# One sequence for neighbourhood and latent attention heads on TensorE, and a token-wise norm for the latent key

## The chip, the cores and the metric

The kernel runs on one core of a Trainium2 chip. The metric is device time in microseconds (us) of one execution; lower is better. The time before is the median of three runs. A profile is one more execution with the hardware profiler on; times in it are counted from the start of its span. Engines are named as in the profile: PE (TensorE matmul), PEld (its weight loads), DVE (VectorE), ACT (ScalarE), POOL (GpSimd), SP (SyncE, which here only issues DMAs).

## The reference, cut to what matters

One encoder layer over 512 tokens with 1024 features. The part that the change touches is the attention: a neighbourhood attention with 8 heads and a latent attention with 8 heads, both fed from one layer-normed input `h`.

```
z = h @ W_in          # columns: NA q | NA k | NA v | c_q (384) | c_kv (256) | k_rope (32)
a_na  = neighbourhood_attention(q_na, k_na, v_na, rpb)        # 8 heads of 64, window 8 x 16, plus bias
q     = rms_norm(c_q, q_norm_g) @ w_uq                        # 8 heads of 64 + 32 (the 32 rotated)
kv    = rms_norm(c_kv, kv_norm_g) @ w_ukv                     # 8 heads of 64 (key) + 64 (value)
a_mla = softmax(concat(q_nope, rope(q_rope)) . concat(k_nope, rope(k_r)) * 96**-0.5) @ v
h     = LN1(alpha * h + concat(a_na, a_mla) @ W_o)
# rms_norm(x, g) = x * rsqrt(mean(x^2) + eps) * g, over the features of a token
```

After it come an expert layer (PEER), a gate and a second LayerNorm, which the change leaves alone.

## The kernel before, in words

Activations lie transposed, features on the 128 partitions and the 512 tokens along the free axis. Every float32 operand of a large product is kept as a high and a low part, and `mm3` (L90 to L92) issues three matmuls for one product. `split` (L75, L76; with a scale L78, L79) makes the two parts: a cast on ScalarE, then a subtraction on VectorE. `stream` loads a weight block through SP's DMA queue into one of three `raw` buffers and splits it into one of two `whi`/`wlo` buffers.

The attention stage's pieces:

- `latent_k(0)`, `latent_k(1)`: the latent key's two halves of 128 features, their squares added up. `rope_key`: the rotated 32-feature key, 24 matmuls and three VectorE operations. `latent_k_norm`: a product with a matrix of ones sums the squares over the partitions and gives every partition the same 512 sums (L298); then VectorE refines the inverse root over 128 x 512 (L300 to L305, four steps of `rsqrt_refine`, L96 to L99), multiplies both halves with it and splits them into `ckh`, `ckl`.
- `na_proj(m)`, m = 0 to 3: queries and keys of a pair of neighbourhood heads, 16 steps of three matmuls. `latent_q(i)`, i = 0 to 2: 8 steps each, with squares added into `sq_q`. `latent_q_scale`: the sums of `sq_q` by token (L330) and their inverse roots `rq`, `nrq`. `latent_values`: 8 steps; it also puts the rotated key into place with DMAs on POOL's queue and clears rows with POOL's memsets.
- `mla_proj(m)`, m = 0 to 3: queries and keys of a pair of latent heads, 5 steps, and before an even m `rope_q`, 6 steps, whose result goes into place by DMAs on POOL's queue.

`run_heads` writes TensorE's order out by hand. It goes over 32 units (pair m, block of 128 queries b, head hh) as a pipeline: in iteration i it issues the scores of unit i + 2, then some steps of the `feeds` (the generators above), then the transposition of unit i's probabilities (L191), and after every second unit the product with the values. The number of feed steps per iteration is the rate: 2.5 (`FEED_NA`) for the neighbourhood heads, 1.2 (`FEED_LAT`) for the latent ones. A feed has a due pair: what is due is driven to its end right before that pair's first scores. A generator's last operations, such as the splits, are issued only when the next step is asked for.

There are two calls of `run_heads`, one for the neighbourhood heads and one for the latent heads; both stand in regions in which TensorE's order is kept as written. `mla_proj(0)` stands between them, outside. The other engines' orders are chosen by the scheduler.

Memory that matters here: PSUM banks come from pools, two banks named `pj` (all projections), two `mm` (scores), two `tr`, two `hp` (head products, and every third latent score). A new tile waits until the bank's last reader is done. `p_exp` and `p_t` have four buffers each in SBUF. The pool `p1` holds the neighbourhood stage's values, bias tiles and projections; after it is closed, `w2h`/`w2l` (half of `W_o`) and the rotated queries `qrh`/`qrl` take its room.

Of the kernel before, what the change touches and what calls it, by code (L numbers as in the profile page):

```python
# [51 lines left out]
def tile_encoder_layer(ctx: ExitStack, tc: tile.TileContext, A: dict, out: bass.AP):  # L52
# [140 lines left out]
        nc.scalar.copy(pT[:, :nk], ps[:, :nk])  # L193
        return pT

    def run_heads(scores, product, feeds, rate, nk):

        ids = [(m, b, hh) for m in range(4) for b in range(4) for hh in range(2)]  # L200
        probs, pts = {}, {}
        fed = 0.0

        def step():
            while feeds:
                if next(feeds[0][1], feeds) is not feeds:
                    return True
                feeds.pop(0)
            return False

        for i in range(-2, len(ids) + 1):
            if i + 2 < len(ids):
                u = ids[i + 2]
                while feeds and feeds[0][0] <= u[0] and step():
                    pass
                probs[u] = scores(*u)
            fed += rate
            while fed >= 1:
                step()
                fed -= 1  # L220
            if 0 <= i < len(ids):
                pts[ids[i]] = transposed(probs.pop(ids[i]), nk)
            if i >= 2 and i % 2 == 0:
                m, b, _ = ids[i - 1]
                product(m, b, [pts.pop((m, b, hh)) for hh in range(2)])
        while step():
            pass

# [64 lines left out]
            nc.vector.tensor_tensor(sq, sq, lat[-1][1], op=OP.add)  # L293
        lat.append((cg, sq))

    def latent_k_norm(lat):
        ss = ps_tile("pj")
        nc.tensor.matmul(ss, ones, lat[-1][1], start=True, stop=True)  # L298
# [4 lines left out]
        nc.vector.reciprocal(sd, sd)  # L303
# [21 lines left out]

    def latent_q_scale():

        ss = ps_tile("pj")
        for c in range(4):
            nc.tensor.matmul(ss[:, c:c + 1], sq_q[:, c * 128:(c + 1) * 128], ones[:, 0:1], start=True, stop=True)  # L330
        yield
        ve = small.tile([128, 4], F32, name="q_ve")
        nc.vector.tensor_scalar(ve, ss[:, 0:4], 1.0 / 384, EPS, op0=OP.mult, op1=OP.add)
        sd = small.tile([128, 4], F32, name="q_sd")
        nc.scalar.sqrt(sd, ve)
        nc.vector.reciprocal(sd, sd)
        rsqrt_refine(rq, sd, ve, ve)
        nc.vector.tensor_scalar(nrq, rq, -(QD ** -0.5), None, op0=OP.mult)
        nc.vector.tensor_scalar(rq, rq, QD ** -0.5, None, op0=OP.mult)

    def rope_key():
        w = stream(A["w_kr"].rearrange("(k p) n -> p k n", p=128), [8, 64])
# [87 lines left out]
                yield  # L430
            nc.scalar.copy(v_mla[:, c, :], ps)

    feeds = []
    for m in range(1, 4):
        feeds += [(m, na_proj(m)), (4, latent_q(m - 1))]
    feeds += [(4, latent_q_scale()), (4, latent_values())]
    with tc.manual_schedule(engines={nc.tensor.engine}):
        lat_k = []
        for part in (latent_k(0, lat_k), latent_k(1, lat_k), na_proj(0), rope_key()):
            for _ in part:  # L440
# [7 lines left out]
    ow = p3.enter_context(tc.tile_pool(name="ow", bufs=1))  # L448
    w2h = ow.tile([128, 8, 512], F32R, name="w2h")
    w2l = ow.tile([128, 8, 512], F32R, name="w2l")  # L450
    p2 = ExitStack()
    lw = p2.enter_context(tc.tile_pool(name="lw", bufs=1))

    qrh = [lw.tile([128, T], F32R, name=f"qrh{r}") for r in range(2)]
    qrl = [lw.tile([128, T], F32R, name=f"qrl{r}") for r in range(2)]

    def q_proj(ps, w, off):
        for k in range(3):
# [4 lines left out]
    def rope_q(r):  # L463
        w = stream(A["w_qr"][:, r * 256:(r + 1) * 256].rearrange("(k p) n -> p k n", p=128), [3, 256])
        px, py = ps_tile("pj"), ps_tile("pj")
        yield from q_proj(px, w, 0)
        yield from q_proj(py, w, 128)
        t1 = lw.tile([128, T], F32, name="qr_t1")
        t2 = lw.tile([128, T], F32, name="qr_t2")
        nc.vector.tensor_tensor(t1, px, cosT, op=OP.mult)  # L470
        nc.vector.tensor_tensor(t2, py, sinT, op=OP.mult)
        nc.vector.tensor_tensor(t1, t1, t2, op=OP.add)
        split(qrh[r], qrl[r], t1)

    def mla_proj(m):
        if m % 2 == 0:
            yield from rope_q(m // 2)
        b = m % 2
        w = stream(A["w_qn"][:, m * 128:(m + 1) * 128].rearrange("(k p) n -> p k n", p=128), [3, 128])
        psq = ps_tile("pj")  # L480
        yield from q_proj(psq, w, 0)
        w = stream(A["w_uk"][:, m * 128:(m + 1) * 128].rearrange("(k p) n -> p k n", p=128), [2, 128])
        psk = ps_tile("pj")
        for k in range(2):
            mm3(psk, (w[0][:, k], w[1][:, k]), (ckh[:, k, :], ckl[:, k, :]), k == 0, k == 1)
            yield
        for par in range(2):
# [9 lines left out]
    n_sc = 0  # L497
# [30 lines left out]
    def load_w2():  # L528
        for kk in range(4):
            raw = wst.tile([128, 2, 512], F32, name="raw", bufs=3)  # L530
            nc.sync.dma_start(raw, A["w_o"][kk * 256:(kk + 1) * 256, 512:1024].rearrange("(k p) n -> p k n", p=128))
            split(w2h[:, 2 * kk:2 * kk + 2], w2l[:, 2 * kk:2 * kk + 2], raw)
        yield

    for _ in mla_proj(0):
        pass
    with tc.manual_schedule(engines={nc.tensor.engine}):
        run_heads(mla_scores, mla_product, [(m, mla_proj(m)) for m in range(1, 4)] + [(4, load_w2())], FEED_LAT, 512)
    p2.close()


    lnp = p3.enter_context(tc.tile_pool(name="lnp", bufs=1))
    lg = row_bcast(lnp, A["ln1_g"], "lg")
# [491 lines left out]
```

## Time and profile before

| | |
|---|---|
| median of 3 runs | 1671.72 us (1669.95 to 1673.59) |
| the profiled execution's own time | 1672.38 us |
| its span, first to last instruction | 1670.6 us |
| mean granted TensorE clock | 0.990 |
| PE, DVE, ACT, POOL busy | 96%, 79%, 44%, 23% |
| first neighbourhood scores, first latent scores | at 73.93 us, at 194.45 us |

A row of the timeline has start, duration, engine, line, operation, what is written from what, shapes, count, and in brackets the engine's idle time before it with what ended it. A row of the waits has who waited, for whom, and total, count and longest in us. Matmul rows show 0.39 us for a 512-column matmul, but they overlap: the next starts 0.23 us later at full clock. The granted clock is given as a share of full speed. Idle time of an engine costs only where TensorE, which is busy nearly all the time, has to wait for it.

### The profile page before, as it was taken

How to read it: one execution, taken by the hardware profiler on the slowest of the kernel's cores; microseconds unless marked ns; L12 is line 12 of the kernel's file. 1: busy time of each engine (PE TensorE's matmuls, PEld its weight loads, DVE VectorE, ACT ScalarE, POOL GpSimd, SP SyncE). 2: the span in 40 equal slices, each digit the busy share in tenths (PEclk: the TensorE clock that was granted, in tenths of full speed). 3: DMA queues.
4: the chain of work that ended last, by engine and by line, in shares of the span. 5: the costliest groups of instructions: out<-in, count | busy, mean ns of one | idle time of the engine just before them, and what ended most of it. 6: DMA issues, size and time to landing. Idle time of an engine off the chain costs nothing.

```text
span 1670.6 us, 24127 instructions
## 1 busy us (share of the span) xinstructions
PE 1611.0 (96%) x8539; PEld 1423.1 (85%) x8539; DVE 1324.9 (79%) x2869; ACT 730.7 (44%) x1233; POOL 383.4 (23%) x335
## 2 busy tenths in 40 slices
PE   6998899999999999999999999999999999999997
PEld 4777777788778999998999999999999999988886
DVE  7466685689999999967878787887878878867776
ACT  3355675433257486753333333333333333333343
POOL 1013100000000000014434343443444434432200
PEclk9999999999999999999999999999999999999999
DMA  7232141233236554479989999899898998977773
GB/s 223 59 107 77 50 143 38 92 90 88 101 124 214 192 192 176 166 267 340 342 319 325 306 333 342 287 340 319 296 334 306 329 337 306 322 251 255 261 240 116
DMA packets 180888, 376.05 MB, mean 225 GB/s; under 512 B 13216, under 2 KB 99616, under 8 KB 177696
## 3 DMA queue, kind: packets, MB, share of 16 engines
q1 hardware_dynamic: 141216, 234.52, 41.5%
q0 software_dynamic: 39552, 140.00, 24.1%
q8 instruction: 67, 1.10, 0.3%
q14 instruction: 53, 0.43, 0.1%
HBM read 339.61 MB, written 32.51 MB: 223 GB/s over the span
## 4 chain that ended last, share of the span: by engine, by line
PE 82%; DVE 12%; ACT 2%; issue 2%; DMA 1%; SPq 0%; POOL 0%; ACTq 0%; DVEq 0%
PE acc L90 10%; PE acc L92 10%; PE acc L91 10%; PE hp L92 10%; PE hp L90 9%; PE hp L91 9%; PE tr L779 3%; PE mm L90 3%; PE mm L92 3%; PE mm L91 3%; PE pj L91 3%; PE pj L90 3%; PE pj L92 3%; DVE oh_j L774 2%; DVE wlo L76 2%
## 5 line engine op out<-in xcount | busy, mean ns | idle before, releaser
L92 PE MATMUL hp<-hTh,wlo 128*128 128x384 f32 x1024 | 349.3, 341 | 5.1 <-DVE wlo L76 5.1
L90 PE MATMUL hp<-hTh,whi 128*128 128x384 f32 x1024 | 349.2, 341 | 2.3 <-ACT ge L609 2.3
L91 PE MATMUL hp<-hTl,whi 128*128 128x384 f32 x1024 | 348.4, 340 | 0.0
L849 POOL DMA_INDIRECT gat<-in_u_rows_dram,i_sel x128 | 170.6, 1333 | 630.8 <-issue 425.3
L92 PE MATMUL acc<-v_hi,a_lo 128*128 128x512 f32 x756 | 294.5, 390 | 0.0
L90 PE MATMUL acc<-v_hi,a_hi 128*128 128x512 f32 x756 | 294.3, 389 | 0.0
L91 PE MATMUL acc<-v_lo,a_hi 128*128 128x512 f32 x756 | 294.2, 389 | 0.0
L75 ACT CAST whi<-raw 128x1024 fp32r<-128x1024 f32 (+3 forms) x181 | 184.4, 1019 | 234.5 <-PE hp L91 121.0
L76 DVE TENSOR_TENSOR wlo<-raw,whi 128x1024 fp32r<-128x1024 f32 (+3 forms) x181 | 213.1, 1180 | 63.0 <-ACT whi L75 62.5
L75 ACT CAST v_hi<-v_raw 128x1024 fp32r<-128x1024 f32 x126 | 132.4, 1051 | 272.2 <-issue 229.6
L860 POOL DMA_INDIRECT gat<-in_v_rows_dram,i_sel x128 | 174.7, 1365 | 267.4 <-DVE base L862 241.2
L76 DVE TENSOR_TENSOR v_lo<-v_raw,v_hi 128x1024 fp32r<-128x1024 f32 x126 | 154.2, 1224 | 83.5 <-ACT v_hi L75 83.4
L92 PEld LDWEIGHTS hp<-hTh,wlo 128*128 128x128 f32 x1024 | 193.3, 189 | 7.7 <-DVE wlo L76 7.7
L90 PEld LDWEIGHTS hp<-hTh,whi 128*128 128x128 f32 x1024 | 193.3, 189 | 6.0 <-ACT ge L609 2.6
L91 PEld LDWEIGHTS hp<-hTl,whi 128*128 128x128 f32 x1024 | 193.2, 189 | 3.4
L862 DVE SCALAR_TENSOR_TENSOR base<-gat,hdot,base 128x1024 f32<-128x1024 f32 x128 | 164.0, 1282 | 10.7 <-DMA gat<-in_v_rows_dram,i_sel 8.4
L92 PEld LDWEIGHTS acc<-v_hi,a_lo 128*128 128x128 f32 x756 | 142.1, 188 | 30.4 <-DVE a_lo L76 1.3
L851 DVE SCALAR_TENSOR_TENSOR scr<-gat,h 128x1024 f32<-128x1024 f32 x128 | 156.4, 1222 | 12.9 <-DMA gat<-in_u_rows_dram,i_sel 10.6
L91 PEld LDWEIGHTS acc<-v_lo,a_hi 128*128 128x128 f32 x756 | 142.1, 188 | 26.3
L90 PEld LDWEIGHTS acc<-v_hi,a_hi 128*128 128x128 f32 x756 | 141.5, 187 | 26.5 <-ACT a_hi L75 0.7
L75 ACT CAST a_hi<-ge 128x384 fp32r<-128x384 f32 x112 | 57.5, 513 | 211.0 <-DVE ge L918 211.0
L76 DVE TENSOR_TENSOR a_lo<-ge,a_hi 128x384 fp32r<-128x384 f32 x112 | 62.6, 559 | 71.2 <-ACT a_hi L75 71.2
(325 smaller groups left out, 2466.9 us busy)
## 6 DMA issues: line engine op xcount, KB each, us to landing
raw<-in_uT_dram SPq DMA_DIRECT2D x128, 512.0 KB, 6.4
v_raw<-in_v_rows_dram SPq DMA_DIRECT2D x128, 512.0 KB, 6.7
g_dram<-g_st SPq DMA_DIRECT2D x24, 1024.0 KB, 4.5
gt<-g_dram SPq DMA_DIRECT2D x16, 1536.0 KB, 15.1
raw<-in_w_in_dram SPq DMA_DIRECT2D x17, 512.0 KB, 4.0
raw<-in_w_q_dram SPq DMA_DIRECT2D x16, 512.0 KB, 4.1
na_b<-in_na_bias_dram POOLq DMA_DIRECT2D x32, 128.0 KB, 2.3
raw<-in_w_o_dram SPq DMA_DIRECT2D x8, 512.0 KB, 4.8
```

The source lines that it names most:

```text
L75: nc.scalar.copy(hi, src)
L76: nc.vector.tensor_tensor(lo, src, r32(hi), op=OP.subtract)
L90: nc.tensor.matmul(ps, a[0], b[0], start=start, stop=False)
L91: nc.tensor.matmul(ps, a[0], b[1], start=False, stop=False)
L92: nc.tensor.matmul(ps, a[1], b[0], start=False, stop=stop)
L774: nc.vector.tensor_scalar(oj[:, i], iota, eT[:, 1, t0 + i:t0 + i + 1], eT[:, 2, t0 + i:t0 + i + 1], op0=OP.is_equal, op1=OP.mult)
L779: nc.tensor.matmul(ps[:, i * 128:(i + 1) * 128], oj[:, 4 * r + i, :], oi[:, 4 * r + i, :], start=True, stop=True)
L849: nc.gpsimd.indirect_dma_start(out=u[:], out_offset=None, in_=u_rows, in_offset=bass.IndirectOffsetOnAxis(ap=i_sel[:, c, k:k + 1], axis=0))
L851: nc.vector.scalar_tensor_tensor(scr, u, 1.0, h[c], op0=OP.mult, op1=OP.mult, accum_out=hdot[:, c, k:k + 1])
L860: nc.gpsimd.indirect_dma_start(out=u[:], out_offset=None, in_=v_rows, in_offset=bass.IndirectOffsetOnAxis(ap=i_sel[:, c, k:k + 1], axis=0))
L862: nc.vector.scalar_tensor_tensor(base[c], u, hdot[:, c, k:k + 1], base[c], op0=OP.mult, op1=OP.add)
```

## The change

- The two calls of `run_heads` become one over 64 units, first the neighbourhood kind, then the latent kind. The rates become 2.75 and 1.0. `mla_proj(0)` is now a feed like the others, due before the first latent scores. At iteration 32 `p1` is closed and `w2h`, `w2l` are allocated.
- `latent_k_norm` sums the squares by token (`token_sums`, four products with one column), refines the inverse root on a 128 x 4 tile (`rms_refined`, now shared with the query's norm), writes it onto the diagonals of four 128 x 128 blocks, and a product with ones (L325) spreads it over the partitions; the two halves are multiplied with it straight from PSUM. It is cut in two: its first part stands before `rope_key`, its second behind it.
- `latent_values` stands before `latent_q_scale`, no longer after it.
- The rotated queries live in `aTh`/`aTl` (blocks 6 and 7) until the heads' results overwrite them; `rope_q`'s first product goes to a `p_exp` buffer and its second is multiplied in its PSUM bank. The first three latent scores take `mm` banks.

The core of the diff:

```diff
-FEED_NA = 2.5
-FEED_LAT = 1.2
+FEED_NA = 2.75
+FEED_LAT = 1.0
...
-    def run_heads(scores, product, feeds, rate, nk):
-        ids = [(m, b, hh) for m in range(4) for b in range(4) for hh in range(2)]
+    def run_heads(kinds, feeds, at_unit):
+        ids = [(kd, m, b, hh) for kd in range(len(kinds)) for m in range(4) for b in range(4) for hh in range(2)]
...
-                while feeds and feeds[0][0] <= u[0] and step():
+                while feeds and feeds[0][0] <= 4 * u[0] + u[1] and step():
                     pass
-                probs[u] = scores(*u)
-            fed += rate
+                probs[u] = kinds[u[0]][0](*u[1:])
+            fed += kinds[ids[max(0, min(i, len(ids) - 1))][0]][3]
...
+            if i in at_unit:
+                at_unit[i]()
...
-    def latent_k_norm(lat):
-        ss = ps_tile("pj")
-        nc.tensor.matmul(ss, ones, lat[-1][1], start=True, stop=True)
-        ve = aw.tile([128, T], F32, name="p_t", bufs=4)
-        nc.vector.tensor_scalar(ve, ss, 1.0 / 256, EPS, op0=OP.mult, op1=OP.add)
-        sd = aw.tile([128, T], F32, name="p_t", bufs=4)
+    def rms_refined(ss, width):
+        ve = small.tile([128, 4], F32, name="rms_ve")
+        nc.vector.tensor_scalar(ve, ss[:, 0:4], 1.0 / width, EPS, op0=OP.mult, op1=OP.add)
+        sd = small.tile([128, 4], F32, name="rms_sd")
         nc.scalar.sqrt(sd, ve)
         nc.vector.reciprocal(sd, sd)
-        rsqrt_refine(sd, sd, ve, ve)
+        y = small.tile([128, 4], F32, name="rms_y")
+        rsqrt_refine(y, sd, ve, ve)
+        return y
+
+    def token_sums(sq):
+        ss = ps_tile("pj")
+        for c in range(4):
+            nc.tensor.matmul(ss[:, c:c + 1], sq[:, c * 128:(c + 1) * 128], ones[:, 0:1], start=True, stop=True)
+        return ss
+
+    def latent_k_norm(lat):
+        y = rms_refined(token_sums(lat[-1][1]), 256)
+        dg = aw.tile([128, T], F32, name="p_t", bufs=4)
+        for c in range(4):
+            nc.vector.tensor_scalar(dg[:, c * 128:(c + 1) * 128], ident, y[:, c:c + 1], None, op0=OP.mult)
+        yield
+        bc = ps_tile("pj")
+        nc.tensor.matmul(bc, ones, dg, start=True, stop=True)
         for i, (cg, _) in enumerate(lat):
-            nc.vector.tensor_tensor(cg, cg, sd, op=OP.mult)
+            nc.vector.tensor_tensor(cg, cg, bc, op=OP.mult)
             split(ckh[:, i, :], ckl[:, i, :], cg)
+        yield
...
+    qrh, qrl = [aTh[:, 6 + r] for r in range(2)], [aTl[:, 6 + r] for r in range(2)]
...
-        t1 = lw.tile([128, T], F32, name="qr_t1")
-        t2 = lw.tile([128, T], F32, name="qr_t2")
+        t1 = aw.tile([128, T], F32, name="p_exp", bufs=4)
         nc.vector.tensor_tensor(t1, px, cosT, op=OP.mult)
-        nc.vector.tensor_tensor(t2, py, sinT, op=OP.mult)
-        nc.vector.tensor_tensor(t1, t1, t2, op=OP.add)
+        nc.vector.tensor_tensor(py, py, sinT, op=OP.mult)
+        nc.vector.tensor_tensor(t1, t1, py, op=OP.add)
...
-        ps = psH.tile([128, 512], F32, name="hp") if n_sc % 3 == 2 else ps_tile("mm")
+        ps = psH.tile([128, 512], F32, name="hp") if n_sc % 3 == 2 and n_sc > 2 else ps_tile("mm")
...
-    feeds += [(4, latent_q_scale()), (4, latent_values())]
...
-        for part in (latent_k(0, lat_k), latent_k(1, lat_k), na_proj(0), rope_key()):
-        latent_k_norm(lat_k)
-        run_heads(na_scores, na_product, feeds, FEED_NA, NA_KEYS)
-    p1.close()
...
-    for _ in mla_proj(0):
-        pass
-        run_heads(mla_scores, mla_product, [(m, mla_proj(m)) for m in range(1, 4)] + [(4, load_w2())], FEED_LAT, 512)
+    feeds += [(4, latent_values()), (4, latent_q_scale())]
+    feeds += [(4 + m, mla_proj(m)) for m in range(4)] + [(8, load_w2())]
...
+        for part in (latent_k(0, lat_k), latent_k(1, lat_k), na_proj(0)):
+            for _ in part:
+                pass
+        norm = latent_k_norm(lat_k)
+        next(norm)
+        for _ in rope_key():
+            pass
+        next(norm)
+        run_heads([(na_scores, na_product, NA_KEYS, FEED_NA), (mla_scores, mla_product, 512, FEED_LAT)], feeds,
+                  {32: na_done})
```

More of the change, by code (lines that the diff above doesn't have):

```diff
@@ L326, in latent_q_scale @@
     def latent_q_scale():
-        ss = ps_tile("pj")
-        for c in range(4):
-            nc.tensor.matmul(ss[:, c:c + 1], sq_q[:, c * 128:(c + 1) * 128], ones[:, 0:1], start=True, stop=True)
+        ss = token_sums(sq_q)
         yield
[L332 to L339, printed above, removed]
+        y = rms_refined(ss, 384)
+        nc.vector.tensor_scalar(nrq, y, -(QD ** -0.5), None, op0=OP.mult)
+        nc.vector.tensor_scalar(rq, y, QD ** -0.5, None, op0=OP.mult)
     def rope_key():
@@ L431, in latent_values @@
             nc.scalar.copy(v_mla[:, c, :], ps)
-    feeds = []
-    for m in range(1, 4):
-        feeds += [(m, na_proj(m)), (4, latent_q(m - 1))]
-    feeds += [(4, latent_q_scale()), (4, latent_values())]
-    with tc.manual_schedule(engines={nc.tensor.engine}):
-        lat_k = []
-        for part in (latent_k(0, lat_k), latent_k(1, lat_k), na_proj(0), rope_key()):
-            for _ in part:
-                pass
-        latent_k_norm(lat_k)
-        run_heads(na_scores, na_product, feeds, FEED_NA, NA_KEYS)
-    p1.close()
-    p3 = ExitStack()
[L448 to L455, printed above, removed]
+    qrh, qrl = [aTh[:, 6 + r] for r in range(2)], [aTl[:, 6 + r] for r in range(2)]
+    p3 = ExitStack()
+    late_tiles = {}
     def q_proj(ps, w, off):
@@ L486, in mla_proj @@
             yield
+        assert m < 2 or n_sc >= 8 * (m - 1), "the tiles still hold an earlier pair"
         for par in range(2):
@@ L495, in mla_proj @@
                 split(st[par, b][0][rows], st[par, b][1][rows], ps[rows])
-    n_sc = 0
     def mla_scores(m, c, par):
@@ L531, in load_w2, with na_done @@
             nc.sync.dma_start(raw, A["w_o"][kk * 256:(kk + 1) * 256, 512:1024].rearrange("(k p) n -> p k n", p=128))
[L532 removed]
+            split(late_tiles["w2h"][:, 2 * kk:2 * kk + 2], late_tiles["w2l"][:, 2 * kk:2 * kk + 2], raw)
         yield
[L535 to L539 removed]
+    def na_done():
+        p1.close()
+        ow = p3.enter_context(tc.tile_pool(name="ow", bufs=1))
+        for n in ("w2h", "w2l"):
+            late_tiles[n] = ow.tile([128, 8, 512], F32R, name=n)
+    feeds = []
+    for m in range(1, 4):
+        feeds += [(m, na_proj(m)), (4, latent_q(m - 1))]
+    feeds += [(4, latent_values()), (4, latent_q_scale())]
+    feeds += [(4 + m, mla_proj(m)) for m in range(4)] + [(8, load_w2())]
+    with tc.manual_schedule(engines={nc.tensor.engine}):
+        lat_k = []
+        for part in (latent_k(0, lat_k), latent_k(1, lat_k), na_proj(0)):
[8 more added lines that the diff above has]
+                  {32: na_done})
+    w2h, w2l = late_tiles["w2h"], late_tiles["w2l"]
     lnp = p3.enter_context(tc.tile_pool(name="lnp", bufs=1))
```

7 lines of the change are left out of this document (4 added, 3 removed).

## The prediction

> **What bounds the kernel now.** I read the page's engine shares and chain first, then busy time by stretches over the attention stage (cut where TensorE's behaviour changes), then TensorE's waits there, then the timeline around each long wait.
>
> ```profile
> PE 1611.0 (96%) x8539; PEld 1423.1 (85%) x8539; DVE 1324.9 (79%) x2869; ACT 730.7 (44%) x1233; POOL 383.4 (23%) x335
> PE 82%; DVE 12%; ACT 2%; issue 2%; DMA 1%; SPq 0%; POOL 0%; ACTq 0%; DVEq 0%
> ...
> 67.80:92.40 24.60, 18.84 (x77) 13.55 (x75) 19.06 (x39) 10.99 (x20) 2.15 (x4) 0.86 0.24 64
> 92.40:125.30 32.90, 32.90 (x198) 28.27 (x196) 20.50 (x70) 18.03 (x48) 6.45 (x12) 1.00 0.38 110
> 125.30:162.70 37.40, 34.14 (x193) 28.20 (x191) 22.49 (x65) 17.66 (x43) 10.12 (x20) 1.00 0.26 79
> 162.70:174.40 11.70, 6.25 (x30) 5.36 (x29) 7.32 (x20) 5.91 (x12) 4.18 (x9) 0.71 0.25 63
> 174.40:193.10 18.70, 18.70 (x109) 15.65 (x107) 9.38 (x29) 11.50 (x28) 0.51 (x2) 1.00 0.08 21
> 193.10:240.00 46.90, 42.81 (x286) 33.03 (x286) 40.91 (x95) 35.60 (x73) 7.30 (x15) 1.00 0.37 100
> ```
>
> The columns of the stretches are length, then busy time (and count) of PE, PEld, DVE, ACT, POOL, then the granted clock, DMA share and GB/s. TensorE is the bound: 96% busy, 82% of the chain. The change touches only 68 to 240 us. TensorE idles there in four of six stretches, and in two of them the clock falls below 1.00. What follows is bound by TensorE too, so I count what is won here one for one. TensorE's waits from 60 to 240 us, total, times, longest:
>
> ```profile
> PE pj L330 <- DVE sq_q L321: 5.5, 1, 5.5
> PE tr L191 <- DVE p_exp L186: 5.4, 1, 5.4
> PE mm L91 <- DVE na_kl L76: 1.8, 2, 1.1
> PE pj L90 <- DVE hTl L76: 1.8, 2, 1.4
> PE mm L90 <- ACT na_kh L75: 1.4, 2, 0.7
> PE mm L90 <- ACT hTh L75: 1.3, 1, 1.3
> PE tr L191 <- DVE rs L185: 0.6, 1, 0.6
> PE pj L90 <- DVE p_exp L348: 0.3, 1, 0.3
> PE mm L92 <- DMA hTl<-qrl: 0.3, 1, 0.3
> ```
>
> Together 18.4 us. The two long ones leave a half clock behind them; here are those stretches, and a feeding step (three matmuls) slow and fast:
>
> ```profile
> 86.00:92.00 6.00, 5.58 (x17) 4.60 (x18) 4.84 (x14) 3.16 (x7) 0.54 (x1) 0.50 0.34 97
> 170.00:175.00 5.00, 5.00 (x20) 4.31 (x21) 1.48 (x9) 1.54 (x4) 0.00 (x0) 0.56 0.01 3
> 88.83 0.63 PE L90 MATMUL pj<-hTh,whi 128*128 128x512 f32 x1
> 90.11 0.63 PE L90 MATMUL pj<-hTh,whi 128*128 128x512 f32 x1
> 96.05 0.40 PE L90 MATMUL pj<-hTh,whi 128*128 128x512 f32 x1
> 96.75 0.39 PE L90 MATMUL pj<-hTh,whi 128*128 128x512 f32 x1
> ```
>
> A step takes 1.28 us after the wait and 0.70 us normally. The half clock costs 5.58 x 0.50 = 2.8 us and 5.00 x 0.44 = 2.2 us. All that can be won is 18.4 + 5.0 = 23.4 us, less what the new order costs in waits of its own.
>
> **Part 1: the norm and the first transpose.** The first transposition waits 5.4 us because VectorE is busy with the latent key's norm over 512 columns:
>
> ```profile
> 67.89 0.40 PE L90 MATMUL pj<-hTh,whi 128*64 128x512 f32 x1
> 73.47 1.02 PE L298 MATMUL pj<-p_exp,ones 128*128 128x512 f32 x2
> 86.42 0.69 PE L191 MATMUL tr<-ident,p_exp 128*128 128x128 f32 x2 [5.41 <-DVE p_exp L186]
> 169.73 1.87 PE L330 MATMUL pj<-ones,sq_q 128*128 128x1 f32 x8 [5.45 <-DVE sq_q L321]
> 68.98 1.22 DVE L76 TENSOR_TENSOR wlo<-raw,whi 128x1024 fp32r<-128x1024 f32 x1 [3.43 <-ACT whi L75]
> 70.23 0.69 DVE L76 TENSOR_TENSOR na_kl<-pj,na_kh 128x512 fp32r<-128x512 f32 x1
> 76.75 3.33 DVE L303 RECIPROCAL p_t<-p_t 128x512 f32<-128x512 f32 x1
> 80.56 0.67 DVE L96 TENSOR_TENSOR p_t<-p_t 128x512 f32<-128x512 f32 x1
> 86.03 0.34 DVE L186 TENSOR_SCALAR p_exp<-p_exp,rs 128x256 f32<-128x256 f32 x1
> 172.28 0.16 DVE L96 TENSOR_TENSOR q_ve<-q_ve,q_sd 128x4 f32<-128x4 f32 x1
> ```
>
> Removed: the reciprocal (3.33) and five full-width operations of at most 0.67, near 6.5 us of VectorE. Added: six operations of 128x4 (0.16, issued 0.2 apart) and four of 128x128, which no row shows: between the 0.16 of 128x4 and the 0.34 of 128x256, so 0.2 each; 2 us in all. On TensorE the four one-column products are new; their kind stands in the row at 169.73, 1.87 us for eight passes at about half clock, so 0.9 to 1.9, taken as 1.0. The spreading product costs what L298 did (1.02).
>
> A new wait comes with it. `pj` has two banks. Before, rope_key took the bank of the query product, long free. Now the token sums take that one, and rope_key needs the bank of na_proj(0)'s key product, free only when na_kl is written. VectorE does the sums' first operation (0.16), then wlo, then na_kl: 70.92 in the rows above becomes 71.1. TensorE is through the sums at 67.9 + 1.0 = 68.9 and waits 2.3 us. Queued behind it is all of TensorE. The 2 us of small norm work then hides under rope_key (24 x 0.233 = 5.6 us, the 67.89 to 73.47 of the rows), which ends at 76.8; the spreading product ends at 77.8.
>
> Is the first transposition earlier? VectorE has after rope_key eight full-width operations (rotation 3, key products 2, splits 3; 8 x 0.69 = 5.5), then three score maxima (0.47 each), three negations (0.15), a weight split (1.22), a reciprocal (0.16) and the scaling (0.34): 76.9 + 5.5 + 1.4 + 0.45 + 1.2 + 0.5 = about 86.0, hardly before the 86.4 of now. But TensorE is late too, for it did the waiting earlier, and it has an eighth step in front of the transposition (three iterations at 2.75 give 8, at 2.5 gave 7): 77.8 + 6.9 (what it did from 73.9 to 80.8) + 0.7 = 85.4. So 0.6 of the 5.4 us is left, and the wait is cut into 2.3 and 0.6. Neither should halve the clock: the trace has half clock after 5.4 and 5.5 us and none after waits up to 1.4.
>
> Part 1: before 5.4 + 0.3 + 2.8 = 8.5; after 2.3 + 0.6 + 1.0 = 3.9. Gain 4.6 us.
>
> **Part 2: 2.75 steps per unit.** Pairs 2 and 3 need 40 and 64 steps before their first scores. At 2.5 the feed gives exactly 40 and 60, so the last split stands right before the scores (na_kh, na_kl: 1.4 + 1.8 = 3.2 us). At 2.75 it gives 44 and 66: three and two steps (2.1, 1.4 us) cover the splits, which end about 2.2 us after the product. Left: 0.3. Gain 2.9 us. The steps themselves only move.
>
> **Part 3: the seam and the latent heads.** The 5.45 us wait is the query's sums standing straight behind latent_q(2). Now latent_values' eight steps (5.6 us) stand between, and the wait with its 2.2 us of half clock goes. What is late next is found by walking the changed queues with these durations:
>
> ```profile
> 168.35 0.60 ACT L320 ACTIVATE p_exp<-pj 128x512 f32<-128x512 f32 x1 [2.18 <-DVE cql L79]
> 169.46 1.28 ACT L335 ACT_TABLE_LOAD   x1
> 197.16 0.78 ACT L183 ACTIVATE p_exp<-mm,nmx,rq 128x512 f32<-128x512 f32 x1 [1.74 <-DVE nmx L181]
> 164.93 0.94 DVE L76 TENSOR_TENSOR wlo<-raw,whi 128x768 fp32r<-128x768 f32 x1
> 196.18 0.69 DVE L509 TENSOR_REDUCE mx<-mm 128x1 f32<-128x512 f32 x1
> hTh<-qrh POOLq DMA_DIRECT2D x8, 64.0 KB, 3.3
> ```
>
> - latent_values' second tile needs latent_q(2)'s bank, which its Square leaves last. ScalarE has a weight cast, an exponential and five copies or activations of 0.4 to 0.7 in front, 4.6 us; TensorE has 2.9 us of work. Wait 1.7.
> - The rotation's and the first pair's tiles: the two table loads (1.28 each) now lie inside this stretch and push ScalarE back; three short waits, 0.55 + 0.25 + 0.55.
> - mla_proj(1)'s first step, put ahead of the first latent scores, needs the bank of the first pair's queries. VectorE has two weight splits (0.95) and four splits of 0.69, then the handshakes: 4.15 us; TensorE has two steps (1.4). Wait 2.75. The rotated queries' DMAs (3.3 us to landing) run meanwhile and come just in time, so they cost nothing here.
> - rope_q(1)'s first tile needs the bank of mla_proj(1)'s queries: on VectorE it stands behind a whole softmax, another maximum and a weight split, 6.3 us against 4.4 of TensorE work. Wait 1.95.
> - mla_proj(2)'s first tile needs the first rotated product's bank, whose cosine product is queued behind the next maximum (0.69) and scaling (0.5): wait 2.45. Before, the cosine product was issued early.
> - The rest of the heads, VectorE as busy as now: 1.0, from the 0.6 to 1.4 of its waits now.
>
> Sum after: 10.2 + 1.0 = 11.2. Before: 5.5 + 2.2 + 1.8 + 1.3 + 0.6 + 0.3 = 11.7. Gain 0.5 us: the seam closes, but its waits come back, smaller and spread out. SP's queue now holds the LayerNorm rows ahead of pair 3's weights and waits there for the neighbourhood's memory; pair 3's weights are wanted some 25 us later, so that costs nothing; without that slack it would cost one landing of 3 to 5 us.
>
> **Sum.** 4.6 + 2.9 + 0.5 = 8.0 us. The profiled execution took 1672.4 us (span 1670.6), 0.7 above the median of the runs; 1672.4 - 8.0 = 1664.4 for a profiled one, and 1671.7 - 8.0 = 1663.7 us for the median.
>
> **Rivals.** *More:* the walk of part 3 strings seven bank waits together, each a difference of two sums; if each queue is a microsecond quicker than I made it, 6 to 7 us of the 10.2 go: 1657. For it: the 1.7 and the three short ones hang on ScalarE's order alone. Against: 40.91 of 46.9 us VectorE is busy in the heads now.
>
> *Nothing to measure:* VectorE becomes the bound from the seam on. It is at 9.38 of 18.7 us before the heads and at 40.91 of 46.9 in them; if the heads run at VectorE's pace, what parts 1 and 2 bring forward is waited for there, some 6 us: 1670. This is also the case in which the sequence is unbroken only in the program.
>
> *Slower:* the new waits of 2.3, 2.75, 1.95 and 2.45 us each halve the clock, as 5.4 did. Each would cost the 2.8 us measured after 86 us: 11.2 - 8.0 = 3.2, and with the 0.6 and 1.7 waits lengthened by slow products about 4 us slower, 1676. It decides where the clock falls: somewhere between 1.4 and 5.4 us of idleness; all four would have to be above that point. [...]
>
> **How the numbers follow.** Chances: forecast (within about 3.5 us) 0.62, more 0.18, nothing to measure 0.13, slower 0.07. A measurement of this kernel tells about 0.2%, 3.3 us, from no change. Faster 0.62 + 0.18 = 0.80, same 0.13, slower 0.07. The range leaves out the slower case and the ends of the outer two: 1656 (more) to 1671 (most of nothing to measure).
>
> **What would show it.** Right: no half clock between 68 and 240 us; first transposition near 86 us with a wait under 1.5; a wait of some 2.3 us at rope_key on na_kl; none before the scores of pair 2; the query's sums without a wait; waits of `pj` on hTl in the heads. Wrong: a clock near 0.5 after any of these, VectorE without a gap from the seam on, or the `pj` waits gone.

## The result, and the profile after

| | before | after |
|---|---|---|
| median, same chip | 1672.65 us (1669.95 to 1674.20, 4 runs) | 1649.59 us (1646.43 to 1654.56, 4 runs) |
| profiled execution, its span | 1672.38, 1670.6 us | 1650.28, 1648.4 us |

The ratio is 0.9867, with a 95% interval from 0.9838 to 0.9895: faster by 23 us, where 8.0 were forecast and the range went down to 1656, 15.7 us below the time before. The direction was right, the size was wrong by a factor of almost three. Two things made it so, and they are of about the same size: the waits that I charged to the new order were nearly twice what they are, and not quite a third of the gain arises in a stage whose code the change does not touch.

Where the 22.2 us between the two spans lie is seen from three landmarks that both traces have: the last product of the latent heads, the last transposition of one-hot rows (the last row of its kind ahead of the expert stage), and the last instruction. First before, then after, from the timeline:

```profile
276.88 1.09 PE L523 MATMUL hp<-p_t,v_mla 128*64 128x128 f32 x14
730.66 1.05 PE L779 MATMUL tr<-oh_i,oh_j 128*128 128x128 f32 x8
1665.42 1.28 DVE L131 SCALAR_TENSOR_TENSOR h<-h,ln_y,gat 128x1024 f32<-128x1024 f32 x1
```

```profile
261.71 1.09 PE L519 MATMUL hp<-p_t,v_mla 128*64 128x128 f32 x14
714.73 1.05 PE L793 MATMUL tr<-oh_i,oh_j 128*128 128x128 f32 x8
1643.24 1.28 DVE L131 SCALAR_TENSOR_TENSOR h<-h,ln_y,gat 128x1024 f32<-128x1024 f32 x1
```

The differences are 15.2, 15.9 and 22.2 us. So 15.2 us come from the attention stage, 0.8 from the 450 us behind it, and 6.2 from the expert stage, whose code is the same in both. (At the expert stage, for each of the 128 blocks of the PEER layer, 24 matmuls write a bank named `hp` and others add to banks named `acc`.)

**The attention stage.** TensorE's waits from 60 to 225 us after, and one behind them; these stand against the 18.4 us of before:

```profile
PE pj L90 <- DVE hTl L76: 3.7, 2, 2.5
PE pj L90 <- DVE p_exp L465: 2.0, 1, 2.0
PE pj L90 <- DVE rms_ve L302: 0.6, 2, 0.3
PE mm L91 <- DVE na_kl L76: 0.6, 1, 0.6
PE pj L90 <- DVE p_exp L363: 0.4, 1, 0.4
PE mm L90 <- ACT na_kh L75: 0.3, 1, 0.3
...
226.34 0.63 PE L191 MATMUL tr<-ident,p_exp 128*128 128x128 f32 x4 [0.71 <-DVE rs L185]
```

The two long ones are gone. The stretch from 60 us to the last product of the heads (busy time by stretches, columns as in the prediction) in the kernel before, in the changed kernel, and in the changed kernel with its tiles at the old addresses (an experiment below):

```profile
60.00:277.70 217.70, 199.05 (x1202) 158.61 (x1200) 149.72 (x390) 128.95 (x279) 30.70 (x60) 0.97 0.30 85
```

```profile
60.00:262.53 202.53, 194.30 (x1212) 156.87 (x1210) 143.53 (x394) 127.94 (x279) 30.63 (x60) 0.99 0.31 92
```

```profile
60.00:261.82 201.82, 193.62 (x1213) 155.86 (x1211) 143.41 (x394) 127.86 (x279) 30.71 (x60) 1.00 0.32 92
```

Idle time is the length less PE's busy time: 18.65, 8.2 and 8.2 us. PE is busy for 10.8, 3.4 and 0 us at a granted clock of 0.50; what the half clock costs is half of that: 5.4, 1.7 and 0. The rest is work: 193.6, 192.6 and 193.6 us. So with tiles at the same addresses nothing of the attention stage's gain is less work: it is 10.45 us of idleness and 5.4 us of half clock, 15.9 in all. The 1.0 us by which the work of the changed kernel is shorter goes with its addresses, for it is gone in the third row.

**The expert stage.** One group of 24 hp matmuls of it, first and last start, before and after:

```profile
1005.03 0.34 PE L90 MATMUL hp<-hTh,whi 128*128 128x384 f32 x1
...
1009.09 0.34 PE L92 MATMUL hp<-hTh,wlo 128*128 128x384 f32 x1
```

```profile
1003.29 0.34 PE L90 MATMUL hp<-hTh,whi 128*128 128x384 f32 x1
...
1007.28 0.34 PE L92 MATMUL hp<-hTh,wlo 128*128 128x384 f32 x1
```

A step is the time from the start of one matmul to the start of the next. 23 steps take 4.06 us before and 3.99 after. Over the whole stage the mean step at full granted clock is 0.1767 and 0.1734 us, with the same instructions; TensorE is idle for 2.7 us before and 2.3 us after, up to the stage's last matmul, and both have one stretch of 3.41 us at half clock. Some 2200 steps of hp, 3.3 ns shorter each, are 7.2 us; as many steps of acc are 0.5 ns longer each, 1.1 us. That is the 6.2 us, nearly. Nothing in the prediction allowed for it.

### The profile page after: what moved, and what is told of

It is laid out like the page before. It is cut to its first block, busy times and chain, and to the rows that moved or that the text cites. A ratio compares the mean times of both kernels' runs of the same rounds, so it can differ in the third digit from the quotient of the medians.

```text
span 1648.4 us, 24146 instructions
## 1 busy us (share of the span) xinstructions
PE 1599.4 (97%) x8547; PEld 1414.1 (86%) x8547; DVE 1318.0 (80%) x2873; ACT 729.9 (44%) x1233; POOL 391.6 (24%) x335
## 4 chain that ended last, share of the span: by engine, by line
PE 85%; DVE 10%; ACT 1%; DMA 1%; issue 1%; SPq 0%; ACTq 0%; DVEq 0%
PE acc L92 10%; PE acc L90 10%; PE acc L91 10%; PE hp L92 10%; PE hp L90 10%; PE hp L91 10%; PE mm L90 3%; PE pj L90 3%; PE pj L91 3%; PE pj L92 3%; PE mm L91 3%; PE mm L92 3%; PE tr L793 3%; DVE oh_j L788 2%; DVE wlo L76 1%; PE tr L191 1%
## 5 line engine op out<-in xcount | busy, mean ns | idle before, releaser
L863 POOL DMA_INDIRECT gat<-in_u_rows_dram,i_sel x128 | 175.4, 1370 | 622.1 <-issue 424.2
L874 POOL DMA_INDIRECT gat<-in_v_rows_dram,i_sel x128 | 178.1, 1392 | 261.3 <-DVE base L876 230.7
```

Of the source, the lines that this page charges most:

```text
L863: nc.gpsimd.indirect_dma_start(out=u[:], out_offset=None, in_=u_rows, in_offset=bass.IndirectOffsetOnAxis(ap=i_sel[:, c, k:k + 1], axis=0))
L874: nc.gpsimd.indirect_dma_start(out=u[:], out_offset=None, in_=v_rows, in_offset=bass.IndirectOffsetOnAxis(ap=i_sel[:, c, k:k + 1], axis=0))
```

## The experiments

Times are medians, beside 1672 to 1674 us for the kernel before on the same chip; "gain" is against that. "Expert stage" is from the last one-hot transposition to the end, 939.2 us before and 932.9 after.

**What moved the expert stage: addresses.** The change puts three small tiles of 128 x 4 where two stood. A buffer of such a tile holds 16 bytes of a partition and takes 32 in the built program; with four buffers that is 128 bytes more (the high part of the streamed weights goes from byte 80608 to 80736 of a partition), and every tile allocated later (`raw`, `whi`, `wlo`, all pools of the later stages) begins 128 bytes higher in its partition. Two kernels test that from both sides.

```diff
+    pad = small.tile([128, 4], F32, name="pad")     # in the kernel before
+    nc.vector.memset(pad, 0.0)
```

> The kernel before with one more small tile (four buffers of 128 x 4, written once), which moves every later SBUF tile, the streamed weights among them, up by 128 bytes, as the change does; nothing else. Some 6.3 us of the 22.2 us by which the two profiled spans differ arise in the expert stage, whose code is the same, by a matmul step of hp of 0.1728 instead of 0.1768 us. Theory A (the place in SBUF sets the pace): the hp step falls to about 0.173 us, the time falls by about 6 us to 1666. Theory B (the pace is the chip's or the execution's, or hangs on TensorE's own instruction stream): the step stays near 0.177 us, the time within 2 us of the kernel before.

Measured: 1665.65 us (1664.62 to 1666.70), ratio 0.9953 (0.9939 to 0.9967), gain 7.3 us; expert stage 932.9 us, hp step 0.1734 us.

```diff
-        sd = small.tile([128, 4], F32, name="rms_sd")        # in the changed kernel
+        sd = small.tile([128, 4], F32, name="rms_sd", bufs=2)
-        y = small.tile([128, 4], F32, name="rms_y")
+        y = small.tile([128, 4], F32, name="rms_y", bufs=2)
```

> The changed kernel with two of its new small tiles in two buffers each instead of four, so that raw, whi, wlo and all later tiles lie where they lay before. Theory A: the hp step of the expert stage returns to about 0.177 us and the time rises by about 6 us over the changed kernel, to some 1656. Theory B: no difference from the changed kernel, about 1649.6.

Measured: 1656.55 us (1656.15 to 1659.10), ratio 0.9903 (0.9887 to 0.9918), 7.0 us slower than the changed kernel; expert stage 939.1 us, step 0.1767 us. Theory A holds on both sides, theory B is out. Here is the count of TensorE's matmuls (the first x) in 400 us of the stage, for the padded kernel before and then for the changed one at the old addresses:

```profile
1000.00:1400.00 400.00, 400.00 (x2037) 365.32 (x2036) 324.71 (x374) 145.36 (x194) 173.47 (x132) 1.00 0.92 322
```

```profile
1000.00:1400.00 400.00, 400.00 (x2022) 366.30 (x2021) 321.79 (x367) 144.40 (x194) 174.00 (x129) 1.00 0.92 320
```

The kernel before has x2022 there and the changed one x2036: the count goes with the address, not with the change. At the old addresses the change is worth 16.4 us.

**The three parts alone**, at the old addresses.

```diff
-        for part in (latent_k(0, lat_k), latent_k(1, lat_k), na_proj(0), rope_key()):
+        for part in (latent_k(0, lat_k), latent_k(1, lat_k), na_proj(0)):
...
-        latent_k_norm(lat_k)
+        norm = latent_k_norm(lat_k)        # token_sums, rms_refined, diagonal product
+        next(norm)
+        for _ in rope_key():
+            pass
+        next(norm)
```

> The kernel before with part 1 alone: token-wise norm in two halves around the rotated key; rates, order and the two sequences as before, tiles of the stream at the old addresses. The prediction: gain 4.6 us, 1668. What the trace of the changed kernel shows (the first transposition without a wait, full clock after it, rope_key waiting 0.35 us and not 2.3): 5.4 + 0.3 + 2.8 less 0.35 and 0.95 = 7.2 us, about 1665. Rival: without the rate of 2.75 TensorE has one step less in front of the first transposition, so 0.7 us of wait stay there: 6.5 us.

Measured: 1667.16 us (1663.78 to 1670.01, 8 runs), ratio 0.9963 (0.9950 to 0.9976), gain 5.8 us. The interval is a gain of 4.0 to 8.4 us, so the time does not choose between the 4.6, 6.5 and 7.2 us that were named; the waits do. Of the wait at the first transposition 0.6 us is left, as the rival said, and rope_key waits 0.3 us and not 2.3:

```profile
PE tr L191 <- DVE p_exp L186: 0.6, 1, 0.6
...
PE pj L90 <- DVE rms_ve L299: 0.3, 1, 0.3
```

```diff
-FEED_NA = 2.5
+FEED_NA = 2.75
```

> The kernel before with part 2 alone: 2.75 steps per unit instead of 2.5. The prediction: gain 2.9 us (the waits on na_kh and na_kl ahead of the scores of pairs 2 and 3 go, 0.3 left). By the trace of the changed kernel 0.85 us are left at pair 3: 2.4 us. One more step ahead of the first transposition takes up to 0.7 us of the 5.4 us wait as well: up to 3.6 us. Rival: the query's sums stay straight behind latent_q(2) and now wait longer, since they are reached earlier: gain near 0.

Measured: 1669.49 us (1667.79 to 1671.24, 9 runs), ratio 0.9978 (0.9968 to 0.9988), gain 3.4 us. The waits on na_kh and na_kl fall from 3.2 to 0.9 us, those of the first transposition and of the query's sums from 5.4 and 5.5 to 5.0 and 4.3. So some 1.6 us of this gain come off two waits that parts 1 and 3 take away as well:

```profile
PE tr L191 <- DVE p_exp L186: 5.0, 1, 5.0
PE pj L330 <- DVE sq_q L321: 4.3, 1, 4.3
...
PE mm L91 <- DVE na_kl L76: 0.6, 1, 0.6
...
PE mm L90 <- ACT na_kh L75: 0.3, 1, 0.3
```

```diff
-    feeds += [(4, latent_q_scale()), (4, latent_values())]
+    feeds += [(4, latent_values()), (4, latent_q_scale())]
```

> The kernel before with one thing of part 3 alone: latent_values stands ahead of the query's sums. The prediction: the 5.5 us wait and the 2.2 us of half clock behind it go, 1.7 us come back at latent_values' second tile: gain 6.0 us. By the trace of the changed kernel that second tile does not wait: gain 7.7 us. Rival: the sums now stand last before the seam, and the first latent exponential needs their inverse roots; what is won is waited for between the two sequences: gain under 2 us.

Measured: 1666.09 us (1665.84 to 1667.42), ratio 0.9958 (0.9945 to 0.9972), gain 7.4 us. The 5.5 us wait is gone from the list and nothing of its size has come in its place; the rival is out. One small wait is new: latent_values' second tile waits for the copy of the first, which is late on ScalarE here (in the changed kernel it is not):

```profile
PE pj L90 <- ACT v_mla L431: 1.0, 1, 1.0
```

**The single sequence.** First the changed kernel at the old addresses, with the swap undone.

```diff
-    feeds += [(4, latent_values()), (4, latent_q_scale())]
+    feeds += [(4, latent_q_scale()), (4, latent_values())]
```

> The changed kernel with its tiles at the old addresses (1656.6 us) and with the query's sums straight behind latent_q(2) again, as before; one sequence, rates and norm stay changed. If the swap carries part 3 (5.5 us wait and 2.2 us half clock, 7.2 us left for part 3 when the measured 5.8 of part 1 and 3.4 of part 2 are taken from 16.4): the time rises by 6 to 8 us, to about 1663. If the single sequence carries it (other work between the sums and latent_q(2) is already there): it stays within 2 us of 1656.6.

Measured: 1664.03 us (1660.88 to 1665.65), 7.5 us slower than with the swap (7.0 by the two gains, each against the kernel before on its own chip). The swap carries part 3. The query's sums wait again, 4.2 us:

```profile
PE pj L314 <- DVE sq_q L343: 4.2, 1, 4.2
```

Then the three parts without the single sequence: the kernel before with the three edits above, at the changed kernel's addresses.

```diff
-FEED_NA = 2.5
+FEED_NA = 2.75
...
-    feeds += [(4, latent_q_scale()), (4, latent_values())]
+    feeds += [(4, latent_values()), (4, latent_q_scale())]
...
+        next(norm)
+        for _ in rope_key():
+            pass
+        next(norm)
```

> The kernel before with the new norm, 2.75 steps per unit and the swap, and with its tiles at the changed kernel's addresses (high part of the weights at byte 80736), but still in two sequences with mla_proj(0) between them and the latent rate of 1.2. If the parts add up and the single sequence brings nothing (5.8 + 3.4 + 7.4 = 16.6 against 16.4 us measured for the whole at the old addresses): 1649 to 1651 us, as the changed kernel. If the single sequence is what lets them add up: slower than the changed kernel by 3 us or more.

Measured: 1649.33 us (1648.23 to 1650.42), ratio 0.9855 (0.9837 to 0.9872): the time of the changed kernel (1649.59). The unbroken sequence, from which the change has its name, brings nothing that can be measured here. The four runs of the changed kernel spread over 8 us, so a difference of 2 or 3 us would not show in the medians; in the two profiled executions, which have the same length of half clock up to there, the last one-hot transposition starts at 714.73 us with it and at 715.61 us without. Its waits are only other ones. Without it, latent scores wait for the first pair's split (3.25 us, the row below), and the mean granted clock is 0.95 from 150 to 185 us and 0.96 from 185 to 225; with it, mla_proj(1) waits 2.49 us for the same splits.

```profile
177.90 0.61 PE L90 MATMUL mm<-hTh 96*128 96x512 f32 x1 [3.25 <-ACT hTh L75]
```

The sum closes: 5.8 + 3.4 + 7.4 = 16.6 us against 16.4, and 7 us of address make the 23. That it closes to 0.2 us is partly chance: each gain is known to about 2 us, the 1.6 us of part 2 that come off the waits of parts 1 and 3 are counted twice, and the 1.0 us that the swap alone leaves at latent_values is counted against it.

**What it is about the addresses.** Six more places. The first kernel leaves 128 bytes free behind the streamed weights, so that those stay and all later tiles move; the others move all tiles of the changed kernel from `raw` on, by n bytes.

```diff
+    padp = ctx.enter_context(tc.tile_pool(name="padp", bufs=1))      # behind wst, in the kernel before
+    pad = padp.tile([128, 32], F32, name="pad")
...
+    pad = small.tile([128, n // 4], F32, name="pad", bufs=1)         # in the changed kernel
```

> The kernel before with 128 bytes left free behind the streamed weights: raw, whi, wlo stay where they are, everything after them moves up by 128 bytes. If the place of the weights sets the step of the expert stage's hp matmuls: it stays at 0.1767 us, and the time near 1672.9. If the place of something else does: 0.1734 us and 1666.

> The changed kernel with all tiles from raw on 32 bytes higher: the streamed weights' high part begins at byte 80768 of a partition, a multiple of 128 (before: 80608, changed: 80736, both 96 above a multiple of 128). If the expert stage's step hangs on whether the weights begin at a multiple of 128 bytes: another step than 0.1734 us, and by 3400 hp and 2200 acc matmuls some 3.4 or 2.2 us for each thousandth of a us. If only the distance from the kernel before counts, as 128 bytes: no difference.

> The changed kernel with all tiles from raw on 160 bytes higher: the weights' high part begins at byte 80896, a multiple of 512. If the place modulo 256 bytes sets the step (before 224 and 0.1767 us, changed 96 and 0.1734 us), this and the kernel with 32 bytes differ from each other as those two do, by about 6 us; if multiples of 128 are as good as each other, both come out alike.

> The changed kernel with all tiles from raw on 64 bytes higher (192 above the kernel before). Steps of the expert stage's hp matmuls seen so far: 0.1767 us at 0 and 160 bytes above the kernel before, 0.1734 us at 128 and 288. If only the place modulo 256 counts and its lower half is the fast one: weights at 160 modulo 256, slow, 0.1767. If there is no such order: any other value.

> The changed kernel with all tiles from raw on 128 bytes higher, 256 above the kernel before. If the effect repeats every 256 bytes: the step and its pattern of the kernel before, 0.1767 us, expert stage 939 us. If it goes on with the distance: another.

> The changed kernel with all tiles from raw on 192 bytes higher (320 above the kernel before; weights at 32 modulo 256). Lower half of 256 fast: 0.1734 us, expert stage 933 us.

Measured, by bytes above the kernel before:

| moved | time, us | hp step, us | acc step, us | expert stage, us | matmuls, 1000 to 1400 us |
|---|---|---|---|---|---|
| 0 (before; changed at old addresses) | 1672.9; 1656.6 | 0.1767 | 0.2268 | 939.2; 939.1 | 2022; 2022 |
| 128 (padded before; changed) | 1665.7; 1649.6 | 0.1734 | 0.2273 | 932.9; 932.9 | 2037; 2036 |
| 160 (after_pad32) | 1657.5 | 0.1767 | 0.2268 | 938.7 | 2020 |
| 192 (after_pad64, one run) | 1655.5 | 0.1744 | 0.2284 | 938.3 | 2026 |
| 256 (after_pad128, one run) | 1657.8 | 0.1767 | 0.2269 | 939.6 | 2021 |
| 288 (after_pad160) | 1653.6 | 0.1735 | 0.2285 | 933.5 | 2028 |
| 320 (after_pad192, one run) | 1660.4 | 0.1755 | 0.2274 | 940.0 | 2023 |
| 128, behind the weights only | 1670.1 | 0.1748 | 0.2276 | 934.2 | 2027 |

The stages at 288 bytes and with the weights left in place lack the one stretch of half clock that the other stages of the table have (3.41 us, which costs 1.7); with it they would be some 935 and 936 us.

Two things follow. At 256 bytes the step is that of the kernel before, and the places at 160 and 288 differ as 0 and 128 do (hp 0.1767 and 0.1735): this fits a repeat every 256 bytes. But only one place, 256, tests the repeat, with one run, and 288 is not as good as 128 in all: its acc step is the longest of the table, and its kernel is 4 us slower than the changed one. And the layouts of before and after show two patterns of steps within a group, each of them to within a nanosecond in most groups (82 and 86 of 87): 176 to 178 ns throughout at 0; 177, 176, 173, 169, 170, 176 and then 173 to 174 throughout at 128. My guess that the lower half of 256 bytes is the fast one failed twice (192: 0.1744 us where 0.1767 was expected; 320: 0.1755 where 0.1734 was). So did the weights' own place as the only cause: hp's operands are the weights and `hTh`, `hTl`, none of these moved with the pad behind the weights, and the step still changed, from 0.1767 to 0.1748 us. Which tile it is, and by what mechanism, stays open.

**Can the waits that are left be taken away?** In the first kernel their banks' readers are issued earlier; in the second the first latent pair also ends three units earlier.

```diff
-        px, py = ps_tile("pj"), ps_tile("pj")
+        px = ps_tile("pj")
         yield from q_proj(px, w, 0)
-        yield from q_proj(py, w, 128)
...
         nc.vector.tensor_tensor(t1, px, cosT, op=OP.mult)
+        py = ps_tile("pj")
+        yield from q_proj(py, w, 128)
...
+        # mla_proj: both query splits directly behind q_proj(psq), ahead of the key's weights
```

> The changed kernel, with the readers of two pj banks issued earlier: the rotation's cosine product right behind its three steps, and the query splits of mla_proj right behind the query's three steps, ahead of the key's weights. If the three waits left in the heads (2.5 and 1.2 us on hTl, 2.0 us on the cosine product) are waits for the issue order alone: they go, with the half clock that follows the first in some executions: 1649.6 - 5.7 = 1644 us, or 1642. If VectorE's total work sets the pace there (34 of 40 us busy), the waits come back at the scores or the transpositions: 1648 or more.

Measured: 1649.64 us (1648.61 to 1651.90), no gain. The 2.0 us wait on the cosine product went, half of it came back at a transposition; the 2.5 us wait stayed, since the splits wait for VectorE, which is at work all the while (its rows follow one another from 171.81 to 175.90 us, and the wait ends at 175.42), and not for their issue:

```profile
PE pj L90 <- DVE hTl L76: 3.8, 2, 2.5
PE tr L191 <- DVE rs L185: 1.7, 2, 1.1
```

```diff
-FEED_NA = 2.75
+FEED_NA = 3.125
...
+        for _ in range(2 if m else 8):          # end of mla_proj: empty steps
+            yield
```

> The kernel after_early with 3.125 steps per unit instead of 2.75 in the neighbourhood heads, so that mla_proj(0) ends three units ahead of the first latent scores, with eight empty steps behind it (two behind the other pairs), and with the due loop ending with the due generator instead of running one step of the next. If the 2.5 us wait is VectorE's time for the rotation and four splits with no TensorE work in front: it goes, 2 to 4 us less than the changed kernel, about 1646. If VectorE's work as such is the bound around the seam: the wait moves to the transpositions, and the time stays at 1649 to 1650.

Measured: 1648.11 us (1647.62 to 1648.95), ratio 0.9855 (0.9839 to 0.9871): 1.5 us less than the changed kernel, with intervals that overlap. The seam's waits went, as expected, but weights now come late (the rows below): no version here is clearly faster than the changed kernel.

```profile
PE pj L92 <- DVE wlo L76: 2.4, 1, 2.4
PE tr L191 <- DVE rs L185: 1.6, 2, 1.1
PE mm L90 <- ACT p_exp L183: 1.1, 1, 1.1
PE pj L90 <- ACT v_mla L446: 0.9, 1, 0.9
```

## Why the prediction was right and wrong, step by step

**Right: what can be won, and where.** The 18.4 us of waits and the half clock (5.0 counted, 5.4 by the clock's rows) are what the change lived on. "One for one" held over the 450 us behind the heads: 15.2 us at their end, 15.9 at the last one-hot transposition. Part 1 was forecast at 4.6 and measured at 5.8 us, part 2 at 2.9 and 3.4, each to about 2 us. These two sizes are partly luck: part 1 holds a wait that did not come (below), and part 2 left 0.9 us of its own waits and not 0.3, and took 1.6 us off two others.

**Wrong: the walk of the banks.** The step that failed is the 11.2 us of new waits that part 3 charged, together with the 2.3 and 0.6 us of part 1. They are 6.7, 0.35 and none. I let the two `pj` banks take turns. In the built program of the kernel before they do, all 42 tiles through; in the changed kernel three tiles of 43 do not. rope_key takes the bank of the token sums, latent_values' second tile that of the first, and the rotation's first tile that of the query's sums. In all three it is the bank whose last reader is done first in the trace. At rope_key the rows show it: it waits for the sums' reader and starts while na_kl is still to be written.

```profile
68.89 0.16 DVE L302 TENSOR_SCALAR rms_ve<-pj 128x4 f32<-128x4 f32 x1 [3.22 <-PE pj L314]
69.20 0.41 PE L90 MATMUL pj<-hTh,whi 128*64 128x512 f32 x1 [0.35 <-DVE rms_ve L302]
70.23 0.68 DVE L76 TENSOR_TENSOR na_kl<-pj,na_kh 128x512 fp32r<-128x512 f32 x1
82.99 0.44 PE L191 MATMUL tr<-ident,p_exp 128*128 128x128 f32 x2
```

The 2.3 us are 0.35, and with rope_key 2 us earlier VectorE's chain behind it is too; the chain itself is some 1 us shorter than I added up. The first transposition stands at 82.99 without a wait (forecast 86.0, wait 0.6). latent_values' second tile likewise: it takes the bank of the first, whose copy is done, and starts ahead of the Square that I made it wait for.

```profile
154.08 0.57 ACT L446 COPY v_mla<-pj 128x512 f32<-128x512 f32 x1
155.15 0.39 PE L90 MATMUL pj<-whi,ckh 128*128 128x512 f32 x1
155.28 0.60 ACT L342 ACTIVATE p_exp<-pj 128x512 f32<-128x512 f32 x1
```

The other terms, forecast and measured: three short waits 1.35 and 0.26 (the rotation's first tile, on the sums' reader); mla_proj(1) 2.75 and 2.49; rope_q(1) 1.95 and 1.20; mla_proj(2) 2.45 and 2.02; the rest 1.0 and 0.71. Pair 3's scores, which part 2 left at 0.3, wait 0.85, and a wait of 0.35 that stood before is there still. So the mechanism was right wherever VectorE's queue was what I walked, a little long each time, and wrong where it was the choice of a bank. In all, 14.4 us of idleness forecast after, 8.2 measured. The remaining difference to 15.9 us: 0.4 of half clock, 0.25 of idleness before, and 1.0 for the sums' matmuls, which I charged, though the work as a whole did not grow (193.64 and 193.62 us).

This is the rival *more*: it said 1657 if the walk's waits were mostly too long, and the changed kernel at the old addresses takes 1656.55. Its chance of 0.18 was too small, for the waits were not independent guesses: one rule for the banks stood behind all of them, and it was wrong for three tiles (the 2.3 us of part 1, and in part 3 the 1.7 and the first of the short ones).

**Wrong: no term for layout.** This is the term that the sum put at nothing, and it is the other 7 us. I took the stages behind the change for unchanged, since their code is. Their addresses are not, and the profile of before could not show what another address does. With a term of plus or minus 7 us for moved tiles the range would have gone down to 1649 and just held the time.

**The other rivals.** *Nothing to measure* needed VectorE without a gap from the seam on; it has gaps (2.29 us before its first maximum of a latent score), and it was the limit only at the waits named above. *Slower* had a true core: of its four waits, three are there (2.49, 1.20 and 2.02 us), and behind the first the profiled execution has a granted clock of 0.50 from 175.56 to 178.97 us, at a cost of 1.7 us and not 2.8; that no half clock would stand between 68 and 240 us was wrong by that. The profile of before has no wait between 1.4 and 5.4 us in this stage, so what waits of this length do to the clock was not shown when the chance of 0.07 was given: it was my estimate.

## What the runs showed of the hardware

**When the clock fell.** In the profiles of before and after every stretch at a granted clock of 0.50 between 60 and 1600 us is 3.41 or 6.83 us long, and within a profile the starts lie whole multiples of 3.41 us apart: at 85.70, 167.62, 467.99 and 758.12 us before (24, 88 and 85 times), at 175.56, 452.04 and 742.17 us after (81 and 85 times). They do not stand at a fixed place to the wait: the half clock begins 0.7 and 2.1 us before the end of the waits of 5.41 and 5.45 us before, and 0.2 us behind the end of the 2.49 us wait after. Windows of 3.41 us counted from these starts, around the 2.49 us wait in the changed kernel, and two windows of that length around the same wait (2.5 us) in the changed kernel at the old addresses:

```profile
168.73:172.14 3.41, 3.41 (x17) 2.53 (x16) 2.76 (x8) 2.22 (x6) 0.00 (x0) 1.00 0.25 76
172.14:175.56 3.42, 0.93 (x5) 0.49 (x4) 3.39 (x7) 2.62 (x6) 2.83 (x6) 1.00 0.72 214
175.56:178.97 3.41, 3.41 (x9) 2.64 (x9) 1.08 (x3) 0.00 (x0) 1.08 (x3) 0.50 0.47 113
178.97:182.38 3.41, 3.41 (x21) 2.93 (x21) 2.03 (x5) 3.03 (x6) 0.00 (x0) 1.00 0.06 22
```

```profile
172.11:175.53 3.42, 1.76 (x8) 1.05 (x6) 2.77 (x6) 3.01 (x7) 1.81 (x4) 1.00 0.67 182
175.53:178.94 3.41, 2.60 (x12) 2.18 (x13) 2.19 (x4) 0.55 (x1) 2.11 (x5) 1.00 0.82 183
```

In the first, the wait falls into one window, which is left with 0.93 us of matmuls, and the next window runs at 0.50. In the second, 1.76 and 2.60 us of matmuls are left in the two windows, and the mean granted clock is 1.00 in both and 1.00 from 185 to 280 us. Cut into such windows between 60 and 1600 us, the profiles of before and after have seven full-clock windows with 0.00 to 1.53 us of matmuls, all followed by half clock, and none with 2.06 us or more that was (some 65 of these had idle time). Nothing in these two lies between 1.53 and 2.06 us. So the same wait cost 1.7 us in one kernel and nothing in the other, and 0.93 us of work in the window did not help. How long the half clock lasted goes with the windows too: of the half-clock windows of the two profiles, the four with 1.30 to 2.69 us of matmuls were followed by another, the seven with 3.17 us or more were not.

**A matmul's step with moved tiles.** At full clock the mean hp step of 384 columns is 0.1767 us in the kernel before and 0.1734 in the changed one, 2% apart. Kernels that differ from these in addresses and in no matmul show it in both directions: 0.1734 in pad128, 0.1767 in after_old_addr.

## What to carry to other kernels

Time a change against itself at the same addresses: 128 bytes more in an early pool moved a 930 us stage by 6.2 us and the kernel by 7 us here, as much as any of the three real edits. When a walk of queues decides a forecast, look up in the built program which bank each tile gets before walking, and count terms that share one rule as one guess. A step that stands straight behind its own producer (the query's sums) was worth more here than the seam around it: moving it behind eight steps of other work gave 7.4 us, and joining the two sequences gave nothing that these runs can tell.
